# Attention with shared key heads: a job loop gives way to a repeating table of steps, and VectorE takes 5 of 32 score tiles

## The chip, the core and the metric

The kernel runs on one core of one Trainium2 chip. The core has five engines that matter here, each with its own queue that it works off in order: TensorE (PE in the profile, its weight loads PEld) multiplies matrices and writes to PSUM; ScalarE (ACT) does the exponentials; VectorE (DVE) does element-wise work; GpSimd (POOL) does element-wise work that does not touch PSUM, and issues the loads; SyncE (SP) issues the stores and the transposing transfers. Engines wait for each other by semaphores. The metric is the device time of one execution in microseconds.

## The reference

There are 8 batches of 512 positions, 32 query heads and 8 key and value heads of dimension 64. Each key head serves four query heads.

```python
scores = np.einsum('bhqd,bhkd->bhqk', Q, K_expanded) * scale
weights = np.exp(scores - np.max(scores, axis=-1, keepdims=True))
weights = weights / (np.sum(weights, axis=-1, keepdims=True) + 1e-10)
output = np.einsum('bhqk,bhkd->bhqd', weights, V_expanded)
```

The order in which the keys are summed does not matter, so long as K and V have the same order.

## The kernel before

The fast path (lines 70 to 506) computes the exponentials without taking the maximum off. It collects evidence that this was allowed (the sums lie between bounds, V is finite), and a general path runs afterwards if it was not; with this input it does not run.

**Tiles.** The unit of work is a *pair*: two query heads that sit in the two halves of the partitions, because a head has 64 dimensions. A pair's scores against 128 keys (index `kc`, 0 to 3) are two matmuls of 512 columns, one per head, into a tile of 128 x 1024 in PSUM (`scores`, L205). There are 128 pairs and so 512 score tiles. A *job* `j` is one key head with its four query heads: two pairs, 8 score tiles. A *unit* `u` is two jobs: two key heads, eight query heads.

**Exponentials.** ScalarE reads a score tile from `s_ps` (two buffers of two PSUM banks) and writes `pt` in fp16 (L227). One tile of eight, the first of the job's second pair, goes another way, over VectorE and GpSimd: *bits* turns the score into the integer that an fp16 power of two has (`u`, L238, from `d_ps`); *mask* keeps its low ten bits (`f`, L259); *slope* and *bend* make a correction from these (`g` and `w`, L251 and L255, on GpSimd for jobs 3 to 62, else on VectorE); *join* adds it and writes `pt` (L272).

**The second product.** For each pair, 32 matmuls (4 key chunks, 2 heads, 4 query chunks) take `pt` as weights and V, with a column of ones, as the moving operand, 65 columns (`pv`, L303). They sum into `pv`, one buffer of two banks. The column of ones gives the sum of the weights. VectorE then takes its reciprocal (L336) and normalises (L340) into `o_sb`; a unit's result is stored in one transfer (L380).

**Other work.** Q is loaded in its natural layout, cast to bf16 on the way, and transposed by TensorE (`trans_q`, L164), 8 matmuls a job into `d_ps`, copied by VectorE (L167). K of batch 0 is transposed likewise (`first_k`), that of later batches by SyncE's transposing transfers (`dma_k`, L151). `check_v` (L177) multiplies V with itself to find values that are not finite, and the bounds of the sums are checked after every 16 pairs (`in_bounds`, L314). K is loaded with one transfer per batch in steady state, V with four, Q with one per unit, all from GpSimd's queue.

**Order.** The program order is written by hand: the loop of L423 places, for each job, its score tiles (`act_tile` 0 to 6 and `exp_d`), and between these parts of the *preceding* job's second product in runs of 11, 11, 10, 16 and 16 matmuls, the normalisations, and the transposes for two jobs ahead. Each engine's instructions stand in this order, and waits follow from tiles and buffers: a buffer's next user waits for the last user of its former content. `d_ps` (one buffer, two banks) serves VectorE's score tiles and the transposes, `pv` the second product alone. PSUM is full: 4 banks `s_ps`, 2 `d_ps`, 2 `pv`.

The two lines that decide VectorE's share, and the loop's core:

```python
return 3 if WIDE(j) else 2                                   # halves of tiles: one tile a job
...
        act_tile(j, 2)
        if late and by_pool(last):
            exp_d4(last)
        exp_d2(j)
        if late:
            pv(last, 0, 11, 22)
```

## Time and profile before

| | us |
|---|---|
| median of 3 runs | 433.32 (433.15 to 433.67) |
| span of the profiled execution | 431.5 |
| ScalarE busy, 448 exponentials | 412.2 |
| TensorE matmuls busy | 392.3 |
| VectorE busy | 309.3 |
| GpSimd busy | 254.1 |
| first exponential starts / last starts / last normalisation ends | 8.44 / 422.67 / 426.91 |
| reads and writes of HBM over the span | 50.33 MB, 33.55 MB |

The profiled execution's span runs from the first to the last instruction; the times of runs include what lies around it, so that the median is 1.8 us above the span.

A page of the profile gives each engine's busy time, the groups of instructions by source line (count, busy time, mean length of one in ns, idle time of the engine just before them and what ended most of it), the chain of waits that ended last, and the transfers. "Busy" of TensorE is modelled from pipelined matmuls whose ends overlap: starts tell more than lengths. The same holds for ScalarE, whose next tile starts before the last has drained.

### The profile page before, as it was taken

The numbers are of one execution on the slowest core, as the hardware profiler recorded it, in microseconds if no ns is written. First come the engines' busy times: TensorE is split into PE (matmuls) and PEld (weight loads), VectorE is DVE, ScalarE is ACT, GpSimd is POOL, SyncE is SP. The second block draws the span as 40 slices with busy tenths as digits, with TensorE's granted clock in tenths as the row PEclk, the third lists the DMA queues.
The fourth block names the chain that finished last, engine by engine and source line by source line (L and its number), as shares of the span: only waits on it lengthen the run. The fifth ranks groups of instructions, "written<-read, shape, count | busy, mean of one in ns | idle before, by whom it ended". The sixth has DMA issues, their size and how long they took to land.

```text
span 431.5 us, 13531 instructions
## 1 busy us (share of the span) xinstructions
PE 392.3 (91%) x5945; PEld 249.6 (58%) x5945; DVE 309.3 (72%) x585; ACT 413.5 (96%) x449; POOL 254.1 (59%) x212
## 2 busy tenths in 40 slices
PE   6889999999999999999999999999999999999984
PEld 2455566556556556556556556566555655655653
DVE  2587778767777767776767876876777776777765
ACT  3889999999999999999999999999999999999993
POOL 8805464965468566595457756497546856545530
PEclk8599999999999999999999999999999999999998
DMA  9998645898649986499946979689954998622214
GB/s 101 173 167 186 171 137 146 124 182 202 154 128 195 143 201 150 119 212 125 259 78 161 191 89 287 149 115 196 204 143 136 187 156 195 151 99 99 99 72 130
DMA packets 91439, 66.97 MB, mean 155 GB/s; under 512 B 52080, under 2 KB 74608, under 8 KB 91376
## 3 DMA queue, kind: packets, MB, share of 16 engines
q0 software_dynamic: 56544, 25.17, 49.9%
q1 hardware_dynamic: 34832, 40.90, 34.9%
q8 instruction: 47, 0.77, 0.7%
q14 instruction: 16, 0.13, 0.1%
HBM read 50.33 MB, written 33.55 MB: 194 GB/s over the span
## 4 chain that ended last, share of the span: by engine, by line
ACT 65%; PE 28%; DVE 4%; issue 1%; POOL 1%; ACTq 0%; DVEq 0%; POOLq 0%
ACT pt L227 65%; PE s_ps L209 12%; PE pv L303 10%; PE d_ps L164 5%; DVE o_sb L340 1%; DVE w L255 0%; DVE pt L272 0%; POOL q_nat L126 0%; DVE qt L167 0%; DVE kt_first L146 0%; PE d_ps L143 0%; DVE g L251 0%; PE d_ps L145 0%; POOL k_nat L103 0%; ACTq L227 0%
## 5 line engine op out<-in xcount | busy, mean ns | idle before, releaser
L227 ACT ACTIVATE pt<-s_ps 128x1024 f16<-128x1024 f32 x448 | 412.2, 1115 | 9.6 <-PE s_ps L209 9.3
L303 PEld LDWEIGHTS <-pt 128*128 128x128 f16 x4096 | 142.8, 98 | 78.2 <-issue 56.1
L303 PE MATMUL pv<-v,pt 128*128 128x65 bf16 x4032 | 178.8, 195 | 3.5 <-DVE o_sb L340 2.5
L209 PE MATMUL s_ps<-qt,kt 64*128 64x512 bf16 x784 | 153.7, 382 | 23.8 <-ACT pt L227 8.6
L251 POOL TENSOR_SCALAR g<-f 128x1024 bf16<-128x1024 int16 x60 | 62.4, 1039 | 154.5 <-DVE f L259 154.5
L255 POOL TENSOR_TENSOR w<-g,f 128x1024 bf16<-128x1024 bf16 x60 | 127.5, 2125 | 5.0
L209 PEld LDWEIGHTS <-kt 64*128 64x128 bf16 x896 | 59.5, 93 | 62.6 <-issue 26.8
L340 DVE TENSOR_TENSOR o_sb<-pv,inv 128x512 f32<-128x512 f32 x125 | 86.4, 691 | 4.3
L336 DVE RECIPROCAL inv<-pv 128x8 f32<-128x8 f32 x125 | 25.7, 206 | 85.4 <-PE pv L303 85.4
L238 DVE TENSOR_SCALAR u<-d_ps 128x1024 int16<-128x1024 f32 x64 | 77.7, 1214 | 0.7 <-PE d_ps L209 0.7
L167 DVE COPY qt<-d_ps 128x1024 bf16<-128x1024 bf16 (+1 forms) x65 | 44.3, 683 | 20.1 <-PE d_ps L177 12.1
L272 DVE TENSOR_TENSOR pt<-u,w 128x1024 uint16<-128x1024 int16 x64 | 43.6, 681 | 0.2
L164 PE MATMUL d_ps<-ident,q_nat 128*128 128x128 bf16 x512 | 40.7, 224 | 0.9 <-DVE kt_first L146 0.9
L164 PEld LDWEIGHTS <-q_nat 128*128 128x128 bf16 x512 | 29.5, 99 | 16.0 <-issue 14.9
L259 DVE TENSOR_SCALAR f<-u 128x1024 int16<-128x1024 int16 x64 | 29.6, 463 | 0.1
L126 POOL DMA_DIRECT2D q_nat<-in_Q_dram x34 | 27.3, 803 | 1.5 <-DMA q_nat<-in_Q_dram 1.2
L111 POOL DMA_DIRECT2D v<-in_V_dram x32 | 28.2, 890 | 0.0
L209 PE MATMUL s_ps<-qt,kt_first 64*128 64x512 bf16 x112 | 24.4, 431 | 2.6 <-ACT pt L227 1.1
L209 PE MATMUL d_ps<-qt,kt 64*128 64x512 bf16 x112 | 21.4, 376 | 0.0
L209 PEld LDWEIGHTS <-kt_first 64*128 64x128 bf16 x128 | 7.6, 96 | 10.8 <-issue 6.5
L177 PE MATMUL d_ps<-v 128*64 128x64 bf16 x256 | 10.4, 201 | 0.0
L177 PEld LDWEIGHTS <-v 128*64 128x64 bf16 x256 | 6.9, 110 | 3.3 <-issue 0.2
(46 smaller groups left out, 52.4 us busy)
## 6 DMA issues: line engine op xcount, KB each, us to landing
out_dram<-o_sb SPq DMA_DIRECT2D x31, 1024.0 KB, 5.9
q_nat<-in_Q_dram POOLq DMA_DIRECT2D x31, 512.0 KB, 7.5
k_nat<-in_K_dram POOLq DMA_DIRECT2D x7, 512.0 KB, 7.7
v<-in_V_dram POOLq DMA_DIRECT2D x28, 128.0 KB, 8.8
kt<-kt SPq DMA_DIRECT2D x14, 256.0 KB, 4.2
out_dram<-o_sb SPq DMA_DIRECT2D x4, 256.0 KB, 2.4
kt<-k_nat SPq DMA_TRANSPOSE x28, 8.7
v<-in_V_dram POOLq DMA_DIRECT2D x4, 96.0 KB, 8.2
```

What stands on the lines that cost most here:

```text
L111: nc.gpsimd.dma_start(out=vt[b % 2][:, sc, lo:hi, 0:D], in_=V[b, sc * 128:(sc + 1) * 128, lo:hi, :],)
L164: nc.tensor.transpose(ps[:, i, sc, :], qn[u][:, sc, h:h + 2, :], ident)
L167: return lambda: nc.vector.tensor_copy(out=qt[u][:, g, lo:hi, :], in_=ps[:, lo:hi, :, :].rearrange("p i sc c -> p i (sc c)"))
L209: nc.tensor.matmul(ps, keys[64 * m:64 * m + 64, g ^ m, kc * 128:(kc + 1) * 128], qt[u][64 * m:64 * m + 64, g, i, :], start=True, stop=True,)
L227: nc.scalar.activation(out=jobs[j]["pt"][:, i, kc, lo:, :], in_=ps[:, lo:, :], func=EXP, scale=scale)
L238: return lambda: nc.vector.tensor_scalar(out=st["u"][:, lo:hi, :], in0=ps[:, 0:hi - lo, :], scalar1=A_U, scalar2=B_U, op0=ALU.mult, op1=AL ...
L251: engine.tensor_scalar(out=g, in0=f, scalar1=-EXP_F1, scalar2=EXP_K * 2.0 ** (24 * as_bits), op0=ALU.add, op1=ALU.mult,)
L255: engine.tensor_tensor(out=w, in0=g, in1=f.bitcast(FP16) if as_bits else f, op=ALU.mult)
L259: nc.vector.tensor_single_scalar(out=st["f"], in_=st["u"], scalar=1023, op=ALU.bitwise_and)
L272: nc.vector.tensor_tensor(out=st["pt"][:, DPAIR, :, :, :].rearrange("p kc m q -> p (kc m) q")[:, 0:n, :].bitcast(U16), in0=st["u"], in1=st ...
L303: nc.tensor.matmul(st["pv"][i][:, m, qc, :], st["pt"][:, i, kc, m, qc * 128:(qc + 1) * 128], vt[b % 2][:, kc, 2 * gp + g, :], start=(n < 2 ...
L340: nc.vector.tensor_tensor(out=osb[u][:, :, h:h + 2, :].rearrange("p qc m d -> p m qc d"), in0=sums[:, :, :, 0:D], in1=inv[:, :, :, None].t ...
```

## The change

The job loop is replaced by a list of tokens, `STEPS`, that describes one *period*: 8 pairs (four key heads, two units). It is walked 16 times and more, and a token with `@1` belongs to the period before, one with `@-1` to the one after, so that neighbouring periods overlap. `Sk` are the matmuls of ScalarE's k-th tile, `Ak` its exponential; `Dk`, `Uk`, `Fk`, `Gk`, `Wk`, `Pk` are scores, bits, mask, slope, bend and join of the k-th tile that VectorE takes; `Vp.lo-hi` is a part of pair p's second product in eighths (four matmuls each); `Rp` and `Np` are its reciprocal and normalisation; `Tk` transposes, `Ck` copies, `Hk` reads the check of V; `Q0` loads Q and `Q1` loads K or V. A trailing `a` or `b` names the PSUM region that a step opens: `a` is `d_ps`, `b` is `pv`. Both now serve second products, VectorE's score tiles and transposes by turns.

- VectorE's share: key chunk 3 of pairs 1, 3, 4, 6 and 7 of each period, 5 tiles of 32, in place of 4 of 32. ScalarE has 27 tiles a period. Pair 1 of the very first period stays on ScalarE.
- Each mask (`F`) stands behind a join (`P`) in VectorE's order. Before, a job's mask followed the preceding job's join too, but the slope and bend had been finished well before.
- Slope and bend run on GpSimd for all but the first and the last unit (`by_pool`); for those they run on VectorE, right behind the mask.
- K is loaded with one transfer per batch whose rows are `p sc` instead of `sc p` (each partition reads four neighbouring rows), V likewise, one transfer per batch in place of four, and Q with one transfer per period (16 heads) in place of two. V has ones in the first and the last column of a pair of heads, so that two heads lie side by side. In the first batch K comes in three and V in four transfers.
- `check_v` has 4 matmuls of 128 columns a unit in place of 8 of 64. The bounds check comes after every 32 pairs on 256 columns, and at the end for 8 pairs at once; the final count and its minimum stand ahead of the last normalisation on VectorE.
- Buffers: Q 3 of double size in place of 4, the VectorE tiles 4 in place of 2.

```diff
-WIDE = lambda j: False
+DVE_KCS = ((), (3,), (), (3,), (3,), (), (3,), (3,))
+STEPS = (
+    "A0 V5.4-5@1 S1 V5.5-8@1 A1 Q1 D0b R5@1 S2 N5@1 W4@1 A2 S3 U0 Q0 T1a A3 S4 H1 C1 "
+    "V6.0-2b@1 A4 V6.2-4@1 P4@1 S5 V6.4-6@1 A5 V6.6-7@1 F0 V6.7-8@1 S6 R6@1 G0 D1a N6@1 A6 "
+    "S7 U1 V7.0-2b@1 W0 V7.2-3@1 A7 V7.3-4@1 S8 V7.4-7@1 A8 V7.7-8@1 S9 R7@1 T2a N7@1 A9 S10 "
+    "C2 A10 P0 S11 D2a F1 V0.0-2b A11 V0.2-3 U2 S12 G1 V0.3-6 A12 V0.6-8 S13 R0 W1 V2.0-1a "
+    "N0 V2.1-2 A13 V2.2-3 S14 V2.3-6 A14 V2.6-8 S15 R2 V1.0-1b N2 V1.1-2 A15 V1.2-4 S16 P1 "
+    "V1.4-6 A16 F2 S17 G2 T3a A17 S18 H3 C3 V1.6-8 A18 W2 S19 R1 D3a N1 A19 S20 U3 V3.0-1b "
+    "A20 S21 V3.1-2 P2 V3.2-4 A21 D4a F3 S22 U4 V3.4-6 G3 A22 S23 V3.6-8 A23 R3 W3 S24 N3 "
+    "T0a@-1 A24 S25 C0@-1 V4.0-4b A25 S26 P3 V4.4-6 V5.0-2a A26 V4.6-8 F4 S0@-1 R4 V5.2-3 G4 "
+    "N4 V5.3-4 "
+).split()
...
-    SPB = 16
+    SPB = 32
...
-    qnat_pool = ctx.enter_context(tc.tile_pool(name="qnat", bufs=4))
+    qnat_pool = ctx.enter_context(tc.tile_pool(name="qnat", bufs=3))
...
-    dve_pool = ctx.enter_context(tc.tile_pool(name="dve", bufs=2))
+    dve_pool = ctx.enter_context(tc.tile_pool(name="dve", bufs=4))
...
-            in_=K[b, :, lo:hi, :].rearrange("(sc p) g d -> p sc g d", p=128),
+            in_=K[b, :, lo:hi, :].rearrange("(p sc) g d -> p sc g d", p=128),
...
-        for sc in range(SC):
-            nc.gpsimd.dma_start(
-                out=vt[b % 2][:, sc, lo:hi, 0:D],
-                in_=V[b, sc * 128:(sc + 1) * 128, lo:hi, :],
-            )
+    def load_v(b, lo=0, hi=GP):
+        nc.gpsimd.dma_start(
+            out=vt[b % 2][:, :, lo:hi, 1:1 + 2 * D],
+            in_=V[b].rearrange("(p sc) (gp g) d -> p sc gp (g d)", p=128, g=2)[:, :, lo:hi, :],
+        )
...
+    def region(tok):
+        return d_tile() if tok[-1] == "a" else pv_tile()
...
+        for sc in range(SC):
+            v = vt[b % 2][:, sc, gp, 1:1 + 2 * D]
+            nc.tensor.matmul(bank[:, 0:2 * D], v, v, start=(sc == 0), stop=(sc == SC - 1))
...
+    def by_pool(n, k):
+        p = n * PPAIR + ON_DVE[k][0]
+        return UPAIR <= p < (NU - 1) * UPAIR
...
+    def pv(p, lo, hi, tok):
+        u, b, gp, g, i = place(p)
         if lo == 0:
+            t = d_tile() if p == NU * UPAIR - 1 else region(tok)
...
+    def last_check():
+        flat = inv_last.rearrange("p s m qc -> p (s m qc)")
+        for n, (bound, op) in enumerate(BOUNDS):
+            nc.vector.tensor_single_scalar(
+                out=right[:, n * LCOLS // 2:(n + 1) * LCOLS // 2], in_=flat, scalar=bound, op=op
+            )
+        count = pv_tile()
+        nc.tensor.matmul(count[0:1, 0, 0:LCOLS + 1], ones, right, start=True, stop=True)
+        nc.vector.tensor_reduce(
+            out=flag, in_=count[0:1, 0, 0:LCOLS + 1], op=ALU.min, axis=AX.X
+        )
...
+    def loads(n, k):
+        b, odd = divmod(n, 2)
+        if k == 0 and n + 2 < NPER:
+            load_q(n + 2)
+        if k == 1 and b + 1 < B:
+            (load_v if odd else load_k)(b + 1)
...
+    for period in range(-2, NPER + 3):
+        for entry in STEPS:
+            tok, _, late = entry.partition("@")
+            n = period - int(late or 0)
+            if 0 <= n < NPER:
+                step(tok, n)
```

More of the change, by code (lines that the diff above doesn't have):

```diff
@@ L244, in by_pool @@
[L244 to L258 removed]
+    every = [(p, kc) for p in range(PPAIR) for kc in range(SC)]
@@ new lines, in fast_path, with on_dve, pt_of @@
+    ON_DVE = [(p, kc) for p, kc in every if kc in DVE_KCS[p]]
+    ON_ACT = [(p, kc) for p, kc in every if kc not in DVE_KCS[p]]
+    def on_dve(n, k):
+        return n * PPAIR + ON_DVE[k][0] >= NPAIR
+    def by_pool(n, k):
+        p = n * PPAIR + ON_DVE[k][0]
+        return UPAIR <= p < (NU - 1) * UPAIR
+    pts, osb, invs, chain, sums, reads, filled = {}, {}, {}, {}, {}, {}, {}
+    def pt_of(p):
+        j = p // NPAIR
+        if j not in pts:
+            pts[j] = pt_pool.tile([128, NPAIR, SC, 2, S], FP16, name="pt")
+        return pts[j][:, p % NPAIR]
```

457 lines of the change are left out of this document (203 added, 254 removed).

## The prediction

> **What bounds the kernel now.** I read the page's engine line and groups first, then the chain of waits, then the timeline of two jobs in the middle, then the windows of the head and the row of one VectorE line.
>
> The page: engines, and the groups that the change touches.
>
> ```profile
> PE 392.3 (91%) x5945; PEld 249.6 (58%) x5945; DVE 309.3 (72%) x585; ACT 413.5 (96%) x449; POOL 254.1 (59%) x212
> ...
> L227 ACT ACTIVATE pt<-s_ps 128x1024 f16<-128x1024 f32 x448 | 412.2, 1115 | 9.6 <-PE s_ps L209 9.3
> ...
> L251 POOL TENSOR_SCALAR g<-f 128x1024 bf16<-128x1024 int16 x60 | 62.4, 1039 | 154.5 <-DVE f L259 154.5
> L255 POOL TENSOR_TENSOR w<-g,f 128x1024 bf16<-128x1024 bf16 x60 | 127.5, 2125 | 5.0
> ```
>
> ScalarE idles 9.6 us in the whole span, 6.3 of them before its first tile. The chain of waits shows its rhythm (start, length, what):
>
> ```profile
> 77.06 6.65 ACT pt L227 x8
> ...
> 89.89 6.65 ACT pt L227 x8
> ...
> 102.72 6.65 ACT pt L227 x8
> ...
> 115.56 2.27 ACT pt L227 x3
> ```
>
> The pattern returns every 12.83 us, which is two jobs of 7 tiles: 0.9166 us per tile. (1115 ns is the latency of one; neighbours overlap.) So in steady state ScalarE sets the pace, and 448 tiles cost 410.6 us. TensorE's slots, in the timeline of a job with a check of V:
>
> ```profile
> 204.96 0.39 PE L209 MATMUL s_ps<-qt,kt 64*128 64x512 bf16 x2
> 205.18 0.39 PE L209 MATMUL d_ps<-qt,kt 64*128 64x512 bf16 x2
> ...
> 208.62 0.39 PE L209 MATMUL s_ps<-qt,kt 64*128 64x512 bf16 x2
> ...
> 208.95 0.62 PE L164 MATMUL d_ps<-ident,q_nat 128*128 128x128 bf16 x8
> ...
> 209.50 0.33 PE L177 MATMUL d_ps<-v 128*64 128x64 bf16 x8
> 209.76 0.39 PE L209 MATMUL s_ps<-qt,kt 64*128 64x512 bf16 x2
> ...
> 211.00 0.67 PE L303 MATMUL pv<-v,pt 128*128 128x65 bf16 x16
> ...
> 211.60 0.39 PE L209 MATMUL s_ps<-qt,kt 64*128 64x512 bf16 x2
> ```
>
> From starts: a score pair takes 0.22 us before another pair and 0.32 before anything else; 16 PV matmuls 0.60 before the next pair (x11 against x16 gives 0.03 each, so 0.03n + 0.12); 8 transposes 0.59; with the V check 0.82. The pair at 209.76 comes 1.14 after its forerunner, 0.22 over the rhythm, the next two stay as late, and ScalarE's 12.83 still holds: **lateness up to 0.23 us is free**.
>
> **The change, part by part.** The work is now a table of 27 ScalarE slots (A0 to A26) for 8 head pairs, in which it was 28.
>
> *ScalarE.* 16 periods x 27 tiles, plus the one tile of pair 1 that it keeps, is 433 instead of 448: 15 x 0.9166 = **-13.75 us**, all on the path, if the others keep up with 27 x 0.9166 = 24.75 us a period (four jobs take 25.66).
>
> *TensorE.* I add up the table between consecutive score pairs: a slot with 8, 12, 16, 20 or 24 PV matmuls takes 0.68, 0.80, 0.92, 1.04, 1.16; with 8 transposes 0.91, and with the new check (4 matmuls of 128 columns at the transposes' 0.056) 1.10; a VectorE tile and 12 PV matmuls 1.02; a VectorE tile alone 0.44; nothing 0.22. The 27 slots sum to 22.0 us of 24.75 (before: 22.3 of 25.66). Order matters more than the sum. Lateness over 0.917 per slot runs up to 0.19 at S4 to S6 (T1 with check), 0.23 at S13 to S16 (V0, V2), 0.18 at S18 (T3) and 0.24 at S0 to S2 (V4, V5), and an idle slot clears it each time. This just fits the measured 0.23. Bounds: nothing lost, or 0.02 to 0.15 us in each of four places (a PSUM region freed late pushes the same slots): 0 to 0.6 us a period, 0 to 9 us. I take 0: the nearest row, 1.14 then 0.92 and 0.92, lost nothing.
>
> *VectorE.* From starts: bits 1.13, join 0.60, mask 0.42, reciprocal 0.24, normalisation 0.61, copy 0.61, check 0.21. A period has 5 x 2.15 + 8 x 0.85 + 4 x 0.61 + 0.4 = 20.4 us of 24.75 (82%; before 18.3 of 25.66). Covered by its idle time.
>
> *GpSimd, and the lap.* 5 x (1.04 + 0.08 + 2.13) = 16.3 us, one Q load 0.81 and one K load 0.75 or V load (16 pieces; rows of 4 and 8 pieces take 0.77 and 0.87, so about 1.1): 18 of 24.75. But each mask now stands behind a join on VectorE, and each join waits for its bend on GpSimd, so join 0.60, mask 0.42, 0.10 to the slope, 1.04, 0.08, bend 2.13, 0.05 back form a closed lap of 4.42. Five make 22.1; the K or V load stands between slope and bend of one lap (+0.9): 23.0 of 24.75. The table places joins at slots 4, 10, 15, 20, 25, so laps have 5 slots (4.58) or 6 (5.50), the load's lap one of 6. Each fits, by 0.15 or more; the PV matmuls that read a join come 3 to 7 slots later, so a single late lap costs nothing. Queued behind a late join are its mask and a reciprocal, which frees a PSUM region.
>
> *Loads.* V issues fall from 34 to 11, K's stay 10, Q's fall from 34 to 19, most of double size. GpSimd's queue is shorter by 38 issues; no engine waits for a load in the steady part of the trace, and none is asked for sooner. K and V rows change order alike. Nothing on the path. SP's queue keeps its stores and transposes.
>
> A row on ports:
>
> ```profile
> L259 DVE TENSOR_SCALAR f<-u x64: 416/418/841, 11.4 to 419.4; 128x1024 int16<-128x1024 int16 x64
> ```
>
> The mask takes 418 ns, but six of 64 take about 835: those beside a V issue on GpSimd. The Q issue now follows the bend, beside join and mask: up to 0.4 us in one lap, in which 1.1 is free. The bounds check, two instructions of 0.28 us on 128 columns after every 16 pairs, becomes two on 256 after every 32 (the rows of 104 and 128 columns differ by 1 ns a column, so 0.41 each), behind the normalisation of pair 7, where a bend has just ended or is ending. I price it at its length, 0.8 us three times, in VectorE's idle time. The Trainium skill, "SBUF — State Buffer" (section "SBUF: two separate sides"), says that a VectorE instruction with two SBUF inputs and a GpSimd one that reads SBUF exclude each other for their whole length. By that rule the check could wait for the bend, up to 2.1 us, and hold the copy behind it, which slot 11 needs about 1 us later: up to 1.2 us lost three times, or 426 us in place of 422.4. No row of this trace has such a check beside a bend.
>
> *Head.* Before, ScalarE's starts run from 8.44 to 422.67; 447 intervals of 0.9166 are 409.7, so 4.5 us are lost, nearly all before 43 us, to a half-clocked TensorE:
>
> ```profile
> 12.50:15.00 2.50, 1.81 (x13) 0.88 (x12) 1.72 (x3) 2.12 (x3) 1.22 (x3) 0.50 1.30 135
> 15.00:17.50 2.50, 2.50 (x19) 0.98 (x15) 2.00 (x4) 2.50 (x3) 2.03 (x6) 0.50 2.19 161
> 17.50:20.00 2.50, 2.50 (x27) 1.41 (x25) 1.08 (x3) 2.09 (x3) 2.50 (x4) 0.50 1.38 201
> 20.00:22.50 2.50, 2.50 (x40) 2.03 (x38) 1.22 (x3) 1.39 (x2) 1.42 (x2) 0.76 1.25 209
> ```
>
> (The column before the last two is the granted clock.) In the new head, by these rows: the first eight transposes between tiles 0 and 3, 0.8 lost; transposes of the second group, 8 of Q and 12 of K in one slot at half clock (8 take 1.03, so 20 about 2.4, and 0.5 for the pair, less 0.92), 2.0; slots 11 to 16, the first with PV matmuls, now at 18.5 us where they began at 16.3, about 1.0 until the clock returns at 21; crowded slots after that 0.5. That is 4.3, about the same: 0 is my value, -1 to +4 the bounds.
>
> *Tail.* Before, the last tile starts at 422.67 and the last normalisation ends at 426.91: 4.2. In the new table four pairs are unsummed at the last tile. Pair 4's sums wait for N3, which stands behind a bits instruction: the last tile slips by about 1.1. After it: join 1.1 (the last three VectorE tiles do slope and bend on VectorE), two reciprocals and normalisations 1.7, waiting for pair 6 and its pair 1.3, reciprocal 0.24, two bounds 0.4, count and minimum 0.5, which now stand ahead of the last normalisation 0.69: 5.9. So **+1.7 and +1.1**.
>
> **Sum**: 431.5 - 13.75 + 2.8 = 420.5 span. The median is 1.8 above the profiled span; 420.5 + 1.8 gives **422.4 us**, 2.5% faster.
>
> **Rivals.**
> 1. *The lap becomes the bound, and the kernel is slower.* For it: it is closed, has three laps with 0.16 us to spare, and VectorE is 82% busy in strict order, so a join can find a 1.13 us instruction ahead of it. Against: 1.7 us free per period. A mean delay of 0.48 per lap makes the period 25.43 and, with the tail's 2.8, eats the whole gain. At 0.6, the half of a bits instruction, 26.0 x 15.5 gives about 442; at 0.4 about 426.
> 2. *TensorE's crowded slots cost ScalarE time.* For it: four places at the edge of the tolerance, 17 changes of PSUM region a period, two regions of one buffer each. 0.2 to 0.6 us a period gives 425.5 to 431.5; it decides the sign only above 0.7.
> 3. *A longer cold head.* At half clock a slot with 16 PV matmuls takes about 1.6 instead of 0.92 (rows of the head: pair to matmuls 0.54, 11 of them 0.72). If the clock returns 3.4 to 14 us later, 0.4 to 4 us more: 423 to 426.5. The skill's "TensorE: Matmul & The Clock Gate", Part 1, has the clock open after a window of about 3.4 us of sustained work; in this trace it opens at about 21 after 6 us without a pause. Until slot 10 the new table leaves TensorE a third idle, so by that rule it opens at 21 or 24.6.
> 4. *The bounds check waits behind a bend* of 2.125 us three times, 1.2 of it on the path: 424 to 426. For it: the check ends up next to that bend. Against: the table has the bend end first.
>
> **Chances.** Forecast (420 to 425) 0.66; rival 1 0.12, two thirds of it slower than before; rival 2 0.13, a quarter of it slower; rival 3 0.06; rival 4 0.03. Under 0.2% (0.9 us, what a measurement can tell from no change) either way: 0.02. Slower 0.13, faster 0.85. The range reaches down to a head and tail without new losses (418.5) and up into rivals 1 and 2: 418.5 to 430.5.
>
> **What would show it.** 433 activations at 0.9166 apart, repeating every 24.75; masks at 418 ns and bends at 2125; last activation to last normalisation 5.9. Wrong if ScalarE shows idle before tiles in every period: released by TensorE after V0, V4 or T1 (rival 2), or with joins that wait long for bends and late reciprocals (rival 1).

## The result, and the profile after

The changed kernel takes **427.74 us** (median; 427.39 to 429.35) beside 433.24 for the kernel before on the same chip: a ratio of 0.9893, interval 0.9867 to 0.9919. It is faster by 5.5 us by these medians and by 4.6 by the ratio (0.0107 of 433.24), where 10.9 were forecast. The sign held and the time lies in the stated range; half of the gain or a little more is missing. The profiled execution has a span of 426.06 us (before 431.47).

The page of the changed kernel, engines and the groups that the change touches:

```profile
PE 382.9 (90%) x5817; PEld 237.7 (56%) x5817; DVE 339.0 (80%) x622; ACT 400.8 (94%) x434; POOL 271.9 (64%) x206
...
L232 ACT ACTIVATE pt<-s_ps 128x1024 f16<-128x1024 f32 x433 | 399.5, 1121 | 13.8 <-PE s_ps L218 13.3
...
L261 POOL TENSOR_TENSOR w<-g,f 128x1024 bf16<-128x1024 bf16 x75 | 159.4, 2126 | 5.5
L253 POOL TENSOR_SCALAR g<-f 128x1024 bf16<-128x1024 int16 x75 | 78.1, 1042 | 121.8 <-DVE f L248 121.8
```

There are 433 tiles on ScalarE as announced, and its idle time has grown from 9.6 to 13.8 us, nearly all behind score matmuls. The chain of waits shows where (start, length, what):

```profile
89.29 5.70 ACT pt L232 x7
...
114.04 5.70 ACT pt L232 x7
...
139.20 5.70 ACT pt L232 x7
...
163.95 5.70 ACT pt L232 x7
```

Distances are 24.75, 25.16 and 24.75: the forecast period, and in one period of four 0.41 more. Taken over the ends of all ScalarE tiles (periods are counted from 0), periods 2, 3, 5, 6, 7, 9, 10, 11, 13 and 14 are 24.75 long, periods 4, 8 and 12 are 25.16, the first two are 29.17 and 26.26, the last is 27.83. That gives this ledger:

| part of the span | before | after | difference | forecast |
|---|---|---|---|---|
| ScalarE tiles at 0.9166 | 448 | 433 | -13.75 | -13.75 |
| start of the first tile | 8.44 | 8.28 | -0.17 | 0 |
| lost in the head (two periods) | 4.78 | 5.93 | +1.16 | 0 |
| middle bounds checks | 0 | 3 x 0.41 | +1.23 | 0 |
| last period beyond 24.75 | 0 | 3.08 | +3.08 | +1.1 |
| end of the last tile to the end | 7.48 | 10.52 | +3.04 | +1.7 |
| sum | 431.47 | 426.06 | -5.41 | -10.95 |

*The lap.* The waits of the changed kernel (in total, times, longest) say that the joins hardly wait for bends, and masks (least, mean, most) are never stretched:

```profile
DVE pt L265 <- POOL w L261: 4.7, 15, 0.4
```

```profile
L248 DVE TENSOR_SCALAR f<-u x79: 416/421/428, 21.1 to 413.4; 128x1024 int16<-128x1024 int16 x79
```

*The middle check.* The timeline of period 4 (start, length, engine):

```profile
120.37 2.12 POOL L261 TENSOR_TENSOR w<-g,f 128x1024 bf16<-128x1024 bf16 x1
...
122.03 0.69 DVE L317 TENSOR_TENSOR o_sb<-pv,inv 128x512 f32<-128x512 f32 x1
...
122.64 0.87 DVE L334 SCALAR_TENSOR_TENSOR ok<-inv,ok 128x256 f32<-128x256 f32 x2
...
123.43 0.68 DVE L178 COPY qt<-d_ps 128x1024 bf16<-128x1024 bf16 x1
...
124.17 0.39 PE L218 MATMUL d_ps<-qt,kt 64*128 64x512 bf16 x2 [0.33 <-DVE qt L178]
```

The check starts 0.15 us after the bend has ended and its two operations take their bare 0.41 us each, but the copy C2 stands behind them, the scores D2 behind the copy, and S12 behind those on TensorE.

*The last period.* Near the kernel's end stands the *early check*: five VectorE operations, 1.3 us, that check the sums of all pairs not yet checked but the last eight, and join the evidence on V to that on the sums. The *last check* takes the last eight pairs and makes the *flag*, the one number that SP loads to decide whether the general path runs. The same view at the largest loss, 1.76 us:

```profile
402.99 0.43 DVE L253 TENSOR_SCALAR g<-f 128x1024 bf16<-128x1024 int16 x1
403.45 0.69 DVE L261 TENSOR_TENSOR w<-g,f 128x1024 bf16<-128x1024 bf16 x1
404.24 0.69 DVE L265 TENSOR_TENSOR pt<-u,w 128x1024 uint16<-128x1024 int16 x1
...
405.05 0.74 DVE L334 SCALAR_TENSOR_TENSOR ok<-inv,ok 128x192 f32<-128x192 f32 x2
...
406.36 0.68 DVE L178 COPY qt<-d_ps 128x1024 bf16<-128x1024 bf16 x1
...
407.10 0.39 PE L218 MATMUL d_ps<-qt,kt 64*128 64x512 bf16 x2 [2.39 <-DVE qt L178]
...
407.75 2.15 ACT L232 ACTIVATE pt<-s_ps 128x1024 f16<-128x1024 f32 x2 [1.65 <-PE s_ps L218]
```

Slope, bend and join (in this unit on VectorE) and the early check stand ahead of the copy C3; TensorE waits 2.4 us for it, ScalarE 1.65. Right after, the granted clock is 0.50 from 408.1 to 411.5 us, and the tiles that follow lose another 1.3.

### The profile page after: what moved, and what is told of

Read it like the earlier page. It is cut to its first block, busy times and chain, and to the rows that moved or that the text cites. A ratio compares the mean times of both kernels' runs of the same rounds, so it can differ in the third digit from the quotient of the medians.

```text
span 426.1 us, 13275 instructions
## 1 busy us (share of the span) xinstructions
PE 382.9 (90%) x5817; PEld 237.7 (56%) x5817; DVE 339.0 (80%) x622; ACT 400.8 (94%) x434; POOL 271.9 (64%) x206
## 4 chain that ended last, share of the span: by engine, by line
ACT 47%; PE 35%; DVE 12%; issue 2%; POOL 2%; ACTq 0%; DVEq 0%; POOLq 0%
ACT pt L232 47%; PE s_ps L218 14%; PE pv L282 11%; PE d_ps L282 4%; PE d_ps L175 4%; DVE u L243 3%; DVE qt L178 2%; DVE o_sb L317 2%; PE d_ps L218 1%; DVE pt L265 1%; DVE okv L187 1%; DVE kt_first L158 1%; PE d_ps L186 1%; POOL w L261 1%; DVE w L261 0%
## 5 line engine op out<-in xcount | busy, mean ns | idle before, releaser
L232 ACT ACTIVATE pt<-s_ps 128x1024 f16<-128x1024 f32 x433 | 399.5, 1121 | 13.8 <-PE s_ps L218 13.3
L261 POOL TENSOR_TENSOR w<-g,f 128x1024 bf16<-128x1024 bf16 x75 | 159.4, 2126 | 5.5
L253 POOL TENSOR_SCALAR g<-f 128x1024 bf16<-128x1024 int16 x75 | 78.1, 1042 | 121.8 <-DVE f L248 121.8
L282 PE MATMUL pv<-v,pt 128*128 128x65 bf16 x3040 | 138.1, 196 | 1.6 <-DVE o_sb L317 1.5
L218 PEld LDWEIGHTS <-kt 64*128 64x128 bf16 x896 | 48.0, 93 | 69.1 <-issue 38.0
L317 DVE TENSOR_TENSOR o_sb<-pv,inv 128x512 f32<-128x512 f32 x90 | 62.2, 692 | 3.1
L265 DVE TENSOR_TENSOR pt<-u,w 128x1024 uint16<-128x1024 int16 x79 | 54.1, 685 | 5.2 <-POOL w L261 4.7
L282 PE MATMUL d_ps<-v,pt 128*128 128x65 bf16 x1056 | 46.3, 195 | 0.0
L317 DVE TENSOR_TENSOR o_sb<-d_ps,inv 128x512 f32<-128x512 f32 x30 | 20.7, 692 | 1.0
L187 DVE TENSOR_REDUCE okv<-d_ps 128x1 f32<-128x128 f32 x32 | 9.3, 291 | 13.2 <-PE d_ps L186 13.2
L243 DVE TENSOR_SCALAR u<-pv 128x1024 int16<-128x1024 f32 x15 | 18.2, 1214 | 0.0
```

Source lines behind the costliest of these rows:

```text
L218: nc.tensor.matmul(ps[:, m, :], keys[64 * m:64 * m + 64, g ^ m, kc * 128:(kc + 1) * 128], qt[u][64 * m:64 * m + 64, g, i, :], start=True, ...
L232: nc.scalar.activation(out=pt_of(p)[:, kc, :, :], in_=filled.pop((p, kc)), func=EXP, scale=scale)
L243: nc.vector.tensor_scalar(out=st["u"], in0=st["ps"], scalar1=A_U, scalar2=B_U, op0=ALU.mult, op1=ALU.add)
L253: engine.tensor_scalar(out=g, in0=f, scalar1=-EXP_F1, scalar2=EXP_K * 2.0 ** (24 * (engine is nc.gpsimd)), op0=ALU.add, op1=ALU.mult,)
L261: engine.tensor_tensor(out=w, in0=g, in1=f, op=ALU.mult)
L265: nc.vector.tensor_tensor(out=pt_of(p)[:, kc, :, :].bitcast(U16), in0=st["u"], in1=st["w"], op=ALU.add)
```

## The experiments

Edits are against the changed kernel. "Span" is that of the profiled execution, a ratio is to the kernel before on the same chip (the changed kernel has 0.9893). Losses are read from the ends of ScalarE's tiles; tile k is the k-th of its period, and a loss is what its distance to the tile before has over 0.9166.

### The last period: slopes to GpSimd (x1), the check later (x2), both (x3)

```diff
 x1, x3
-        return UPAIR <= p < (NU - 1) * UPAIR
+        return UPAIR <= p < NU * UPAIR
 x2, x3
-                if what == "H" and j == 2 * NU - 1:
-                    early_check()
...
                 (inverse if what == "R" else norm)(p)
+                if what == "N" and p == NU * UPAIR - 5:
+                    early_check()
 x3
         nc.vector.reciprocal(out=inv, in_=sums[p][:, :, :, s:s + 1])
-        if left == 1:
-            last_check()
...
             store(u, 0, 2 * HPG)
+        if left == 1:
+            last_check()
```

> The slopes and bends of the last unit (pairs 124 to 127, three tiles) go to GpSimd like all others. In the changed kernel the last period is 27.83 us long instead of 24.75, and 1.76 us of that are one loss at ScalarE tiles 20 and 21, behind the copy C3, which stands on VectorE behind slope, bend and join of the tile of pair 4 (0.43 + 0.69 + 0.69 us) and behind the early check (1.35 us). Theory: work ahead of C3 on VectorE makes that loss. Then 1.8 us less stand ahead of C3, the loss of 1.76 falls under 0.4, the last period is about 26.3 long, and the end of the last tile's chain gives up to 0.4 back (its bend takes 2.1 us instead of 0.7): span 424.5 to 425.3, about 1.2 under 426.1. Rival (the last period is long for another reason, the early check alone or the clock): loss at tiles 20 and 21 stays over 1.2, span 425.8 to 426.6.

> The early check (five VectorE operations, 1.35 us together) runs behind the normalisation of pair 123 instead of ahead of the copy C3 of the last period. Theory (all VectorE work ahead of C3 counts alike): C3 comes 1.35 us earlier, the loss at tiles 20 and 21 falls from 1.76 to about 0.4, and behind pair 123 these operations lie in VectorE's idle time: span 424.6 to 425.2. Rival (slopes and bends alone make the loss, the early check lies beside other work): span 425.8 to 426.4.

> Both of the former (slopes and bends of the last unit on GpSimd, early check behind pair 123), and the last check (bounds, count and minimum of the last pairs) behind the last normalisation instead of ahead of it. Theory: the last period falls to 24.9 to 25.6 us (from 27.83); the last normalisation comes 0.8 us sooner behind its reciprocal, and the last store no longer stands behind the load of the flag on SP (0.5 us), so that the end comes 4 us after the last normalisation or sooner instead of 5.6: span 426.1 - 2.4 - 1.3 = 422.4, between 421.8 and 423.4. Rival (the store's landing of 3.9 us, or the drain, sets the end whatever stands ahead): the last period shortens, but the stretch from the last ScalarE tile to the end stays at 11.6 us, span 423.4 to 424.4.

x1: span 427.0, ratio 0.992 (0.9896 to 0.9944). The theory fails: the loss at tile 20 does not shrink, it grows from 1.76 to 2.90, and the span lies above the rival's too. Its timeline:

```profile
403.53 0.29 DVE L187 TENSOR_REDUCE okv<-d_ps 128x1 f32<-128x128 f32 x1 [0.81 <-PE d_ps L186]
403.74 2.54 DVE L334 SCALAR_TENSOR_TENSOR ok<-inv,ok 128x192 f32<-128x192 f32 x2
403.94 2.13 POOL L261 TENSOR_TENSOR w<-g,f 128x1024 bf16<-128x1024 bf16 x1
...
406.84 0.68 DVE L178 COPY qt<-d_ps 128x1024 bf16<-128x1024 bf16 x1
```

The check that took 0.74 us takes 2.54. Its first operation (0.35) runs; the second starts at 404.12, beside the bend that began at 403.94, and ends at 406.28, 0.2 us after that bend. This is rival 4 of the prediction, here and not in the changed kernel. The Trainium skill, "SBUF — State Buffer" (section "SBUF: two separate sides"), describes this as a lock that whichever starts first holds for its whole length; the row of the second operation agrees. That a bend waits for VectorE is not seen here: it began 0.15 us before the check's first operation ended and kept its 2.13 us.

x2: the loss at tile 20 falls to 0.45 as expected and the period to 26.52. But the span stays at 426.0, the rival's value (ratio 0.9894, 0.9869 to 0.9918): with slopes and bends still on VectorE, TensorE waits 1.4 us for the normalisation of pair 123, the last tile loses 1.13, the clock falls to half at 417.1, and the end comes 12.2 us after the last tile's end instead of 10.5.

x3: span 424.0 (theory 422.4, rival 423.4 to 424.4), ratio 0.9821 (0.9797 to 0.9846). The last period is 24.81, without a loss worth naming:

```profile
404.37 0.29 DVE L187 TENSOR_REDUCE okv<-d_ps 128x1 f32<-128x128 f32 x1 [0.81 <-PE d_ps L186]
404.58 0.68 DVE L178 COPY qt<-d_ps 128x1024 bf16<-128x1024 bf16 x1
...
405.32 0.39 PE L218 MATMUL d_ps<-qt,kt 64*128 64x512 bf16 x2
...
409.39 2.12 POOL L261 TENSOR_TENSOR w<-g,f 128x1024 bf16<-128x1024 bf16 x1
...
410.23 1.89 DVE L334 SCALAR_TENSOR_TENSOR ok<-inv,ok 128x192 f32<-128x192 f32 x2
```

So it takes both: neither VectorE's slope and bend nor the check may stand ahead of C3. The stretch from the last tile's end to the end did not shrink by the 1.3 us expected (10.85 instead of 10.52). Two things ate it: the early check met a bend again (the last row, 1.89 instead of 0.74) and the last tile's bend took 2.1 us on GpSimd. And the end is no longer set by the store: SP's own chain behind the flag (load, compare, a row of waits) ends 3.7 us after the minimum.

### The middle checks: left out (x4), moved (x9, x13)

```diff
 x4
-        if left > NLAST and ((p + 1) % SPB == 0):
-            bulk_check(SPB)
 x9, x13: remembered there as waiting, and run ...
 x9
+                if what == "R" and k == 5 and waiting:
+                    bulk_check(SPB, waiting.pop())
                 (inverse if what == "R" else norm)(p)
 x13
+                if what == "H" and k == 3 and waiting:
+                    bulk_check(SPB, waiting.pop())
                 read(j if what == "C" else (j, "v"))
```

> The three bounds checks of sums in the middle (two VectorE operations of 0.41 us each, behind the normalisation N7 of periods 3, 7 and 11) are left out, so a part of the safety check on the sums is not computed. Theory: these operations by their own length stand ahead of the copy C2, so periods 4, 8 and 12 are 25.16 us instead of 24.75; without them all are 24.75, span 1.2 us shorter, 424.7 to 425.2. Rival 1 (the forecast's own view: they fit into idle time and the 0.41 come from the load of K or V or a late sum): the three periods stay at 25.1, span 425.8 to 426.4. Rival 2 (they wait for a bend): then more than 0.41 a time would come back, span under 424.5.

x4: the chain of waits now has 24.75 across the period that held a check (114.04 to 139.20 in the changed kernel):

```profile
89.00 5.70 ACT pt L232 x7
113.75 5.70 ACT pt L232 x7
138.50 5.70 ACT pt L232 x7
```

Periods 4, 8 and 12 are 24.75 each, 1.23 us regained, so the theory holds in the profile. The span is 425.4 and not 424.8, because TensorE stopped once for 0.63 us (below), which cost 0.67. The ratio, 0.9884 (0.9859 to 0.991), is too coarse to show 1.2 us.

> Nothing is left out: the three bounds checks of the middle run about 17 us later, ahead of the reciprocal R5 of the period after, where VectorE was idle for 0.65 us with no bend on GpSimd (114.64 to 115.30 in the changed kernel's trace). Theory (place, not length, is what the check cost): periods 4, 8 and 12 are 24.75, the three periods that now hold the check lose 0 to 0.17 each, both operations take 0.41 to 0.43 us: span 0.8 to 1.2 shorter than 426.1 for the same head. Rival (0.82 us more of VectorE cost 0.41 wherever they lie): sum of the periods unchanged.

x9 is *slower* than the kernel before: ratio 1.016 (1.0141 to 1.0178), span 437.4. Periods 4, 8 and 12 are 24.75 as hoped, but 5, 9 and 13 are 28.7 to 29.0:

```profile
139.58 3.92 DVE L336 SCALAR_TENSOR_TENSOR ok<-inv,ok 128x256 f32<-128x256 f32 x2
139.83 1.22 POOL L123 DMA_DIRECT2D v<-in_V_dram  x1
141.07 2.13 POOL L261 TENSOR_TENSOR w<-g,f 128x1024 bf16<-128x1024 bf16 x1
```

I had looked up the idle place in an even period, where K's load ends early; the check falls into odd ones. Its second operation begins while GpSimd issues the load of V, and lasts until that issue and the bend behind it are over: 3.43 us for 0.41 us of work. TensorE waits meanwhile, and each time 3.41 us of half clock follow, which are part of the 3.9 to 4.2 us lost.

> Nothing is left out: the three bounds checks of the middle run just ahead of the reduction H3 of the period after, where VectorE was idle for 0.86 us (104.56 to 105.41 in the changed kernel's trace), with no load's issue and no bend on GpSimd (its bend began at 105.72). Theory (place, not length): both operations take 0.41 us each, periods 4, 8 and 12 are 24.75 to 24.95 instead of 25.16, or the slope beside them is held and the next join comes 0.1 to 0.3 us late; no period over 25.0. Rival 1 (the slope or bend gets in first and the check waits for it as in the run before): those periods take 26 us and more. Rival 2 (0.82 us of VectorE cost 0.4 wherever they lie): 25.16 as before.

x13: periods 4, 8 and 12 are 24.76, but 5, 9 and 13 are 25.05 to 25.06 (a loss of 0.3 at tile 8): 0.1 us gained a time, where the theory had no period over 25.0. Span 426.6 with a first period 0.3 longer and a start 0.8 later than the changed kernel's; ratio 0.9885 (0.9865 to 0.9905). The timeline:

```profile
130.38 1.59 DVE L336 SCALAR_TENSOR_TENSOR ok<-inv,ok 128x256 f32<-128x256 f32 x2
130.56 1.15 POOL L253 TENSOR_SCALAR g<-f 128x1024 bf16<-128x1024 int16 x1 [1.78 <-DVE f L248]
131.79 2.17 POOL L261 TENSOR_TENSOR w<-g,f 128x1024 bf16<-128x1024 bf16 x1
```

Even the slope, which reads one tile, holds the second operation (1.14 instead of 0.41 us). The loss comes out at tile 8 of the odd periods, in which V's load stands in the lap. The price of the check is one of place, and neither of the two places tried is free.

### Masks ahead of joins again (x6), V in four loads (x7)

```diff
 x6: each F moved to right behind its U in STEPS, for instance
-    ... A2 S3 U0 Q0 T1a A3 ... V6.6-7@1 F0 V6.7-8@1 ...
+    ... A2 S3 U0 F0 Q0 T1a A3 ... V6.6-7@1 V6.7-8@1 ...
 x7
-        nc.gpsimd.dma_start(
-            out=vt[b % 2][:, :, lo:hi, 1:1 + 2 * D],
...
+        for sc in range(SC) if hi - lo == GP else (slice(0, SC),):
+            nc.gpsimd.dma_start(
+                out=vt[b % 2][:, sc, lo:hi, 1:1 + 2 * D], in_=src[:, sc, lo:hi, :]
+            )
```

> Each mask stands right behind its bits again, ahead of the join of the tile before, and so often while GpSimd is at a bend. Theory (the mask and the bend cannot run side by side, as the bounds check in the run with the last unit on GpSimd lay 2157 ns beside a bend of 2126 instead of 414): masks beside a bend take up to 2.1 us instead of 0.42, by the places of bits and bends in the steady period two or three of five wait 0.3 to 1.3 us, reciprocals, normalisations and copies behind them come late, and the period grows by 0.3 to 1.5 us: 432 to 450, with masks of 0.8 us and more on average. Rival (the mask takes its 0.42 beside a bend; only the long lap from join to mask was meant to be shortened): masks 416 to 430 ns, period 24.75, 427 to 428.

x6: 502.8 us, ratio 1.161 (1.158 to 1.164); the theory's direction, far beyond its size. Groups of x6 (busy, mean ns of one):

```profile
L261 POOL TENSOR_TENSOR w<-g,f 128x1024 bf16<-128x1024 bf16 x75 | 164.1, 2188 | 5.5
...
L265 DVE TENSOR_TENSOR pt<-u,w 128x1024 uint16<-128x1024 int16 x79 | 129.0, 1633 | 0.3
...
L248 DVE TENSOR_SCALAR f<-u 128x1024 int16<-128x1024 int16 x79 | 60.6, 767 | 2.7
```

Masks average 767 ns instead of 421, and joins 1633 instead of 685. The averages hide two kinds: the 15 masks that began beside a bend take 2.2 us and the other 64 their 0.43; the 53 joins that began beside a bend, a slope or a load's issue take 2.1 on average and the other 26, among them 15 that began before a slope, their 0.68. I had counted only the masks: an early mask also lets GpSimd start its next slope and bend early, and then a *join* is caught beside that bend: in its timeline one runs from 110.89 to 113.20, beside a bend from 110.53 to 112.66. With the mask behind the join, the closed lap that the prediction saw as a risk is what keeps bends away from masks and joins. Between 67 and 410 us TensorE's clock also falls to half thirteen times for 3.41 us; how much of the 75 us that makes was not separated.

> V of each later batch comes by four loads instead of one (seven times; each issue about 0.8 us on GpSimd between a slope and its bend, 3.2 instead of 1.22 in all). Theory of the lap (join, mask, slope, bend and the next join follow each other; five laps and a load took 23.0 of 24.75 us): in seven periods the lap takes 25.0 and the join waits for its bend, 0.3 to 0.6 us a time or up to 2 where the next join is on the path: 2 to 8 us slower than the changed kernel, 429.5 to 435.5, and joins that wait 1 us and more for bends. Rival (GpSimd's 6 us of idle time a period take it up): joins wait as before, 0.3 or less a time, 427 to 428.5.

x7: 443.5 us, ratio 1.0256 (1.022 to 1.0292), slower than the kernel before. The odd periods take 1.5 to 2.8 us more than in the changed kernel, most of it at tile 8, and the first of them 3.9 more; together these are the 16.8 us by which its span (442.9) is longer. The waits of x7, and GpSimd's timeline in period 3:

```profile
DVE pt L266 <- POOL w L262: 17.7, 21, 2.1
```

```profile
93.83 3.05 POOL L125 DMA_DIRECT2D v<-in_V_dram  x4
96.86 2.16 POOL L262 TENSOR_TENSOR w<-g,f 128x1024 bf16<-128x1024 bf16 x1
```

Joins wait 17.7 us for bends instead of 4.7. The lap is real and has little room: the issues take 1.8 us more in one of the five laps, and periods 9, 11 and 13, where the clock stays whole, lose 1.5 to 1.6. The four odd periods before them lose more, 2.6 to 3.9, and each has a stretch of half clock behind the wait. The theory had the mechanism and undersized it (2 to 8 us); with four loads the fifth tile does not pay.

### The share alone undone (x8)

```diff
-DVE_KCS = ((), (3,), (), (3,), (3,), (), (3,), (3,))
+DVE_KCS = ((), (3,), (), (3,), (), (), (3,), (3,))
 STEPS: D2 U2 F2 G2 W2 P2 taken out, D3.. and D4.. renumbered, S17 A17 put in
```

> The new table, steps, loads and masks, but the tile of pair 4 stays on ScalarE: 28 tiles there and 4 of 32 on VectorE, as before the change. Theory (the fifth tile brings 15 x 0.9166 = 13.75 us, and the 8.2 us that were lost again belong to the new arrangement: head, three bounds checks, last period, end): 427.7 + 13.75 = 441.4, 8 us slower than before, with the same losses in the head and the last period. Rival (the arrangement costs nothing by itself, the losses come because TensorE, VectorE and GpSimd have less room with the fifth tile): 433 to 435, period 25.66 throughout.

x8: 438.8 us, ratio 1.0143 (1.0124 to 1.0163), between the two expectations. The steady period is 25.67, in periods 4, 8 and 12 too: the middle check is free with 28 tiles and costs 0.41 with 27. The end is dear without the fifth tile as well: the last period is 2.49 longer than 25.67 (at other tiles: 1.76 of it at the last one), and the end comes 11.25 us after the last tile's end (before 7.48). So about 6 us at the end belong to the new arrangement, whatever its share. The clock in its head was half in two pieces of together 10.2 us, not comparable with the changed kernel's 17.1, so it tells nothing on the head.

### The head: TensorE kept busy (x5)

```diff
+    junk = pv_tile()
+    def keep_warm(count):
+        for _ in range(count):
+            nc.tensor.matmul(junk[:, 1, :], warm[:, 0:128], warm, start=True, stop=True)
     for copy in [first_k(0, swap, bank[:, swap, :]) for swap in range(2)]:
         copy()
+    keep_warm(4)
     trans_q(0, 0, d_tile()[:, 0, :], 0, 1)()
+    keep_warm(2)
...
+            if n == 0 and 2 <= k <= 9 and k != 8:
+                keep_warm(2)
```

> 22 matmuls on zeros (128 columns by 512, into a PSUM tile that nothing reads) are added in the first 14 us: four behind the first K copies, two behind the first Q transposes, two behind each of ScalarE tiles 2 to 7 and 9 of period 0. Theory: period 0 loses 4.4 us (29.17 instead of 24.75) because TensorE runs at half clock from 8.8 to 25.8 us, so that the 20 transposes of one slot take 1.97 us and hold the scores behind them; with TensorE kept busy the clock stays up from about 9 to 16 us at least, the losses of 1.48, 1.00 and 0.83 at tiles 10, 12 and 13 shrink to 0.5, 0.3 and 0.2, and the end comes 2 us sooner than the changed kernel's on the same chip. Rival 1 (the losses are waits for copies and loads, the clock does nothing): no loss smaller, end within 0.3 us. Rival 2 (the added matmuls stand ahead of scores and cost their own 0.2 to 0.4 us a tile while the clock falls all the same): 2 to 5 us later.

x5: 426.1 us, ratio 0.9853 (0.9834 to 0.9871). The same stretch of the head, first in the changed kernel and then in x5 (the number before the last two is the granted clock):

```profile
8.40:36.50 28.10, 24.59 (x254) 12.99 (x252) 15.26 (x28) 24.45 (x26) 11.51 (x15) 0.70 0.91 143
```

```profile
8.40:36.50 28.10, 24.76 (x310) 13.20 (x310) 17.14 (x33) 26.30 (x28) 11.68 (x15) 1.00 0.98 172
```

With the clock at 1.00 throughout, ScalarE is busy 26.3 of these 28.1 us instead of 24.5, and period 0 is 27.06 instead of 29.17. The clock's share of the head is 2.1 us, as expected; the span is only 0.8 shorter, 425.3, because TensorE stopped once (below), which cost 1.27. Two losses of period 0 remain. The 0.74 at tile 10 is a slot crowded with transposes of Q and K. The 1.12 at tile 14 is VectorE's: TensorE waits 1.17 us for the bits of a tile, which stand behind mask, slope, bend and join of the tile before, all on VectorE in the first unit. The 1.5 us of period 1, the same in every run with 27 tiles but x6 and x7, lie at slots around transposes and copies of the K groups; no run takes these out.

### The end, and everything together (x10, x11, x12, x14, x15, x16)

```diff
 x10, x12, x14, x15, x16
-        return UPAIR <= p < (NU - 1) * UPAIR
+        return UPAIR <= p < NU * UPAIR - 1
 x11: last_check() behind the last store, as in x3; x10, x12: early_check() there too
 x14, x15, x16: the early check's bounds ahead of H3 of the last period, its rest ahead of
 R of the pair before the last; the last bounds and the count behind the last reciprocal, the
 minimum behind the last normalisation and its store
 x12: x10 with x5 and x9;  x15: x14 with x5 and x13;  x16: x14 with x5
```

> In the last unit GpSimd does slopes and bends of all tiles but the very last, and the early check runs behind the last normalisation with the last check. Theory: no VectorE operation and no bend stand ahead of C3, so the last period is 24.8 to 25.0 (27.83); the last tile has its bend on VectorE in 0.7 us, so the stretch from the last ScalarE tile to the last normalisation is again 5.0 us or less, not 6.3 as with all on GpSimd; the last normalisation comes 0.8 us sooner behind its reciprocal and its store goes out at once: span 426.1 - 3.0 - 0.8 - 0.5 = 421.8, between 421.0 and 422.6 for the same head. Rival (the flag is read 1.4 us later and ends the kernel): 422.6 to 423.6.

> The last check alone is moved behind the last normalisation. Theory: the last normalisation follows its reciprocal at once (0.8 us sooner) and the last store is issued ahead of the load of the flag (0.5 us): the stretch from the last ScalarE tile to the end falls from 10.5 to 9.2 us, span 424.6 to 425.0. Rival (the store's landing varies on its own between 2.4 and 3.9 us and the order does nothing but swap flag and store): 10.0 to 10.6 us, span 425.6 to 426.2.

> The three together, and the 22 matmuls on zeros in the head. Theory (the losses are independent): 426.1 - 1.2 (middle checks) - 4.3 (last period and end) - 2.1 (period 0, 27.06 instead of 29.17) = 418.5 for the span, 417.8 to 419.8, time 419.5 to 421.5. Rival (what is gained ahead is lost to the next wait behind it, above all in the last period): span over 420.5.

x10: span 424.5, ratio 0.9849 (0.9828 to 0.987), with one stop of TensorE in it that cost 1.27; without it 423.3, in the rival's range. The last period is 24.81 and the last normalisation ends 5.4 us after the last tile's end, but the end comes 5.4 us after that: the rival was right, the flag is late and SP's chain behind it (3.3 us here) ends the kernel.

x11: span 426.3 (the slowest of its five runs, with the start 0.8 later than the changed kernel's and half clock from 413.1 to 419.9), ratio 0.9857 (0.9837 to 0.9876). From the last tile's end to the end it takes 9.97 instead of 10.52: the theory's 9.2 is missed, and half clock over the last products leaves open by how much. The last store is issued 0.03 us after its normalisation instead of 0.50, and no longer decides; the flag does, 3.66 us before the end. The store also lands sooner. The pages give the median from issue to landing of the four stores at the end, first for the changed kernel, then for x11:

```profile
out_dram<-o_sb SPq DMA_DIRECT2D x4, 256.0 KB, 3.6
```

```profile
out_dram<-o_sb SPq DMA_DIRECT2D x4, 256.0 KB, 2.3
```

The very last store takes 3.91 us in the changed kernel and 2.31 in x11. All 18 profiles divide alike: in the ten in which it stands behind the load of the flag on SP it takes 3.5 to 4.1 us, in the eight in which it stands ahead 2.3 to 2.4. So the last store's landing goes with the order and does not vary on its own, as the rival had it. Why it is late behind the flag's load stays open, and so does why the three stores before it, ahead of that load in both, take 2.9 to 3.6 us in the changed kernel and 2.3 to 2.7 in x11.

x12: span 434.1, far above the theory's 419.8, ratio 1.0085 (1.0069 to 1.01). It inherits x9's checks (13.2 us in three periods); its head (27.07) and last period (24.80) are as expected.

> Of the early check the bounds run ahead of H3 of the last period, the rest ahead of R6 of the last pairs; GpSimd does all slopes and bends but the last tile's; behind the last reciprocal stand the last bounds (0.3 us) and the count on TensorE, then the last normalisation, then the minimum. Theory (the flag and SP's chain behind it of 3.3 to 3.7 us set the end when the store goes first): last period 24.8 to 25.0, minimum done 1.2 to 1.3 us after the last reciprocal began, end 3.3 to 3.7 us behind it: from the last ScalarE tile to the end 9.0 to 9.6 us instead of 10.5, span 421.7 to 422.6 for the changed kernel's head. Rival (the store's landing of 2.4 to 3.9 us sets the end anyway): end 4.5 us and more behind the last normalisation, 9.7 to 10.6.

> The two before together (middle checks ahead of H3; the end) with the 22 matmuls on zeros in the head. Theory (the losses are independent and add): 426.1 - 0.9 - 4.0 - 2.1 = 419.1 for the span, 418.3 to 420.2; time 420 to 422. Rival (they do not add): over 421 for the span.

> The new end and the matmuls on zeros in the head, with the middle checks left where the change has them. Theory: 426.1 - 4.0 - 2.1 = 420.0 for the span, periods 4, 8 and 12 at 25.16; it lies 0.6 to 1.2 us over the run with the middle checks moved as well. Rival (the moved checks cost more in their new place): it lies under that run.

x14: span 424.0, ratio 0.9824 (0.9798 to 0.985). Behind the minimum 3.40 us to the end, as the theory said; but from the last tile to the end 11.1, outside both expectations. The windows of x14's end show why (TensorE busy first, granted clock before the last two):

```profile
412.90:415.50 2.60, 0.14 (x5) 0.01 (x1) 2.50 (x6) 0.00 (x0) 0.00 (x0) 1.00 0.50 178
415.50:418.90 3.40, 3.28 (x60) 3.29 (x61) 2.35 (x8) 0.00 (x0) 0.00 (x0) 0.50 0.55 154
```

TensorE did next to nothing for 2.6 us, and its last products then ran at half clock. The same code in x15 and x16 has the same lull, kept the full clock and took 9.65 and 9.67.

x15: **422.15 us**, ratio 0.9756 (0.9737 to 0.9775), faster than both kernels, with everything computed that the changed kernel computes; span 421.5, with a start 0.65 later than the changed kernel's and a stop of TensorE that cost 1.07 in period 11 (theory 418.3 to 420.2; the other four runs of x15 have spans of 419.9 to 420.5). x16: 423.3 us, ratio 0.9809 (0.9771 to 0.9847), span 420.0, as forecast. By their ratios these two are not told apart. In x16's profile head and end together bring 6.0 us of span, 2.1 in period 0, 3.0 in the last period and 0.85 behind the last tile, which is the sum of the single gains; so there the losses add. But this profile is the fastest of six runs that spread from 422.0 to 427.2 us, and what the slower ones lost is not known.

## Why the prediction was half right

The pace was right, and what was added to it failed. The steps that failed are two terms of the sum, the last period (+1.1, measured +3.08) and the tail (+1.7, measured +3.04), and two that it put at nothing, the bounds checks (measured +1.23) and the head (measured +1.16). In the last period and at the checks it was VectorE's order: work that was counted as covered, or not placed at all, stood ahead of a copy that TensorE waited for.

*ScalarE, right.* 433 tiles, 0.9166 apart, 24.75 a period, to the digit.

*TensorE's slots, right.* No steady period without a check loses anything; rival 2 is out. Lateness up to 0.24 us per slot was free.

*VectorE's sum, right and misleading.* 20.66 us busy in a period of 24.8, forecast 20.4. It was used to cover things with "idle time", and that step failed, as the next point shows.

*The bounds check, wrong.* "I price it at its length, 0.8 us three times, in VectorE's idle time": the length is right (two operations of 0.41), the cover only by half. VectorE has 4 idle us a period, but the copy behind N7 had about 0.4 to spare, and the other 0.41 came out at ScalarE each time. The text even said that slot 11 needs that copy "about 1 us later", and used it only for rival 4. Measured 1.23, shown by x4. Rival 4 itself did not occur in the changed kernel, by 0.15 us; x1, x9 and x13 show that it is real.

*The lap, right.* Five legs and a load fit; joins waited 0.4 at most. x7 shows that the room is as small as the sum said (23.0 of 24.75), x6 what happens without it. Rival 1 is out for this kernel.

*Loads, right.* No stretched masks, no wait for a load in the steady part.

*The head, undersized.* Forecast 4.3 lost, measured 5.93 beside 4.78. The clock was half from 8.8 to 25.8 us instead of 7.6 to 21.2: rival 3, at the small end of its price. x5 puts the clock's share at 2.1 of it; 1.5 more lies in period 1, where the forecast had "crowded slots after that 0.5", and with a full clock (x5) 1.1 remain at tile 14, behind slope and bend on VectorE, which the sum of the head does not have.

*The last period, the mis-sized term.* Forecast +1.1 through pair 4's sums; measured +3.08, elsewhere: TensorE waits 0.37 us for N3 there and no tile is late by it, and the loss lies at tiles 20 to 23. The prediction knew that slope and bend of the last unit run on VectorE, and charged them only behind the last tile. That they and the early check stand ahead of C3 was not walked through. x1 to x3 show that both must go before the loss goes: 24.81 in x3. Of the 3.08, 1.3 come in the stretch of half clock behind the wait.

*The tail, right as far as it went.* From the last tile's start to the last normalisation 5.99, forecast 5.9. But the sum stopped there. Behind it stood 4.56 us before and 5.56 after: the flag's load now stands ahead of the last store on SP (issued 0.50 us after its normalisation, before 0.03), and that store landed 3.9 us after its issue (before 2.3). x11 and the division of the 18 profiles tie both to this order. The sum put nothing for what stands behind the last normalisation, without a reason; it was 1.0. The remaining 0.3 of the 3.04 is the last tile itself, which lasts 1.03 instead of 1.32 and so leaves more behind its end.

The missing 5.5 us of span are thus 1.2 in the head, 1.2 in the checks, 2.0 in the last period and 1.3 at the end, less 0.2 at the start. The spans of the two runs that mend head and end are shorter by 6.0 (x16) and 4.6 us (x15); 2.1 of that is half clock in the head, which the kernel before has too.

## What to carry to other kernels

An engine's idle time covers an added instruction only if what stands directly behind it in that engine's order has slack: look there, not at the busy share. When work is spread over VectorE and GpSimd, write the order so that work that stays in SBUF on the one never meets a bend or a load's issue on the other, and move such an instruction only after looking at every period it falls into. Walk the last period and the last instructions of each queue as carefully as the steady state: here they held more than half of what was missed.

## What the runs showed of the hardware

- VectorE operations that stay in SBUF (bounds checks and joins of two tensors, masks of one) wait while GpSimd is at a slope, a bend or a load's issue: 2157 ns instead of 348 beside a bend of 2126 (x1), 3425 instead of 414 beside a load's issue and a bend (x9), 1141 beside a slope (x13); joins 1633 instead of 685 and masks 767 instead of 421 on average (x6). For x1 the bare length is 348, not the 414 that the expectation of x6 compares it with; that is for 256 columns. GpSimd's side changes little: bends take 2188 in x6 and 2126 in the changed kernel. VectorE operations that read PSUM keep their time even in x6 (bits 1215 ns, normalisations 692).
- TensorE's clock changes on a grid of 3.41 us: the half-clocked stretch in the head is 17.07 us long, five of these, before the change 13.65, four. The Trainium skill, "TensorE: Matmul & The Clock Gate", Part 1, gives 3413 ns for that window; the trace agrees. How a lull of TensorE lies on this grid matters: in the 18 profiles every lull behind the head with 2.1 us or more in one window was followed by half clock (the 2.39 of the changed kernel's last period; the 2.58 at x14's end, with 2.49 in one window). The same lull at the end of x15 and x16, cut by a window's edge into parts of at most 1.3 and 1.8, was not; some lulls with smaller parts were (x5, x7, x13).
- In five profiles (x4, x5, x8, x10, x15) TensorE stops once for 0.6 to 1.2 us between two instructions (ScalarE loses 0.7 to 1.7), each time near tiles 16 to 19 of an odd period (5, and in x15 11), with no releaser in the profile. In all five it goes on 1.4 to 1.6 us after a transfer of 16 KB of instructions has landed. That points to instructions that came late, but no run tests it.
